# Layer A of a pooling and attention trunk as one stream of units on four PSUM banks

## The chip, the cores and the metric

One core of a Trainium2 chip runs the whole program. The metric is the device time of one execution in microseconds (us). The engines are TensorE (PE, matmuls; PEld is its weight load), VectorE (DVE), ScalarE (ACT), GpSimd (POOL) and SyncE (SP), which issues nearly all DMAs in the order of its queue.

## What is computed

x has 512 positions of 2048 channels. Layer A is a gated pooling mixer, layer B is latent attention on the residual stream. What the change touches is layer A and the norms at the start of layer B:

```python
def pool_mixer_layer(x, norm_g, w_in, w_group, scale, w_out):
    h = rmsnorm(x, norm_g)
    proj = h @ w_in                                   # 2048 -> 2 * 4096
    u, gate = proj[..., :W_A], proj[..., W_A:]
    u = u.reshape(B, S, N_POOL_GROUPS, G_A)           # 4 groups of 1024
    pooled = jnp.stack([causal_mean_pool(u[:, :, gi], w) - u[:, :, gi]
                        for gi, w in enumerate(POOL_WINDOWS)], axis=2)   # windows 2, 4, 8, 16
    y = jnp.einsum('bsgc,gcd->bsgd', pooled, w_group).reshape(B, S, W_A) * scale
    y = y * jax.nn.silu(gate)
    return x + y @ w_out                              # 4096 -> 2048
```

Layer B normalises the new x (shared_kv, mla_layer): an rmsnorm of x, and one each of the key and value latent and of the query latent, both 512 wide.

## The kernel before

Channels lie on the 128 partitions, positions along the free axis; a tile is 128 x 512 in float32. Every float32 operand is split into a rounded high part (a cast on ACT) and a low remainder (a subtraction on DVE), and a product is three matmuls: high by high, high by low, low by high (`mm3`, `split`).

**Seven products for eight.** The products with `w_in` and `w_out` are made for pairs of output tiles by a scheme with seven block products in place of eight. `w_combos` (L278) loads the two weights of a pair for two input pairs (512 KB), forms the sums on DVE (L283) and POOL (L285, L286), casts seven blocks on ACT (L289) and subtracts on DVE (L290). `seven` (L300) issues 21 matmuls of 256 columns for each input pair (L306, L308, L310) into four PSUM banks `k0` to `k3`. `gather` (L313) sums the banks (ACT L317, DVE L318 to L321). The inputs stand split in eight tiles `xh`, `xl`, one for each pair of input tiles, in the pool `xcp`.

**Stages of layer A**, one after the other:
1. A first stage loads x, splits it and multiplies pairs 16 and 17 of the 32 output pairs.
2. The other pairs go in the order `early + late` (L410), four `w_combos` each. Pairs 0 to 15 are u, 16 to 31 the gates. Pairs 18 to 21 go before the norm factor `r2` is known and are stored raw. A pair of u is scaled by `r2` and pooled at once for pairs 0 to 11 (`pool_pair`, one doubling step after the other on DVE, L337, then L343, L344, and a store to DRAM); pairs 12 to 15 are stored and pooled later. Gates go through SiLU and to DRAM. `finish_gates` does that for pairs 16 to 21 later, behind the pools of pairs 0 to 5.
3. `group(g, j0)` (L455) multiplies one pooling group with its own matrix: eight steps, each with a DMA of 512 KB of weights and one of 256 KB of pooled data, a split of 128 x 1536 and 24 matmuls of 512 columns into all eight banks. Then y = product by scale by gate (L477), its block sums (L483 to L485) and splits, as the next `xh`, `xl`.
4. Groups 0 and 1, then the output pass b = 0 over eight pairs (`out_part`, `out_end`): it adds the product to the residual and stores it (L510, L512); pools 12 to 15 are spread over it. Then groups 2 and 3 and the pass b = 1. Each pass starts with the first halves of pairs 0 and 1.

The tiles of weights (`raw` with three buffers, `hi` and `lo` with two) are shared by all these stages.

**Layer B** begins with products of the new x. `norm_r` (L165) makes a norm factor: four float32 products with one column of ones, reciprocal square root by three Newton steps on 128 x 4 (`rsqrt`, L156), then a diagonal matrix and a product that spreads it over the partitions.

**Order.** The program is written as one sequence. A planner orders the instructions of each engine by its own estimate of when each could run, with the written order as priority; so an instruction may be moved ahead of one that waits. Within an engine's queue the result is fixed.

Of the kernel before, what the change touches and what calls it, by code (L numbers as in the profile page):

```python
# [7 lines left out]
F32 = mybir.dt.float32  # L8
# [6 lines left out]
P = 128  # L15
# [36 lines left out]
def trunk_kernel(  # L52
# [128 lines left out]
    def r_tile():  # L181
        return rpool.tile([P, S], F32, tag="r", name="r")
# [56 lines left out]
    tile_ = dict(reuse_waits="tile")  # L239
# [3 lines left out]
    with ExitStack() as c1:  # L243
# [83 lines left out]
        def pool_pair(pair, up, nt):  # L327

            w = WINS[pair // 4]
            G.memset(up[:, :, 0:PAD], 0.0)  # L330
            prev, off = up, PAD
            m = 1
            while m < w:
                ext = w - 2 * m
                nw = S + ext
                nx = nt()
                V.tensor_tensor(nx[:, :, 0:nw], prev[:, :, off - ext:off + S],  # L337
                                prev[:, :, off - ext - m:off + S - m], ALU.add)
                prev, off = nx, ext
                m *= 2  # L340

            rc = cs[:, None, C_RCNT:C_RCNT + w - 1].broadcast_to([P, 2, w - 1])
            V.scalar_tensor_tensor(prev[:, :, 0:w - 1], prev[:, :, 0:w - 1], float(w), rc, ALU.mult, ALU.mult)  # L343
            V.scalar_tensor_tensor(prev[:, :, 0:S], prev[:, :, 0:S], 1.0 / w, up[:, :, PAD:],  # L344
                                   ALU.mult, ALU.subtract)
            raws[pair] = dram()
            nc.sync.dma_start(raws[pair], prev[:, :, 0:S])
# [40 lines left out]
        c3 = ExitStack()  # L388
        tp[0] = c3.enter_context(tc.tile_pool(name="tpool1", bufs=3, **tile_))
        rp = c3.enter_context(tc.tile_pool(name="rp", bufs=1, **tile_))  # L390
# [17 lines left out]
        early = (18, 19, 20, 21)  # L408
        late = (22, 0, 8, 23, 1, 9, 24, 2, 10, 25, 3, 11, 26, 4, 12, 27, 5, 13, 28, 6, 14, 29, 7, 15, 30, 31)
        for n, pair in enumerate(early + late):  # L410
            ks = banks()
            for q in range(NJ // 2):
                w = w_combos(*(awin[2 * pair + m][:, q * S:(q + 1) * S] for m in range(2)))
                seven(ks, w, 2 * q)
                seven(ks, w, 2 * q + 1)
# [3 lines left out]
            if n == 4:  # L419
                V.tensor_tensor(sq[:, 0, :], sq[:, 0, :], sq[:, 1, :], ALU.add)  # L420
                p = ps7.tile([P, 2, H], F32, tag="k3", name="k3").rearrange("p h t -> p (h t)")
                norm_r(sq[:, 0, :], D, p, pt()[:, 0, 0:S], [(r2[:, 0, :], 1.0), (r2[:, 1, :], -1.0)])
            v = gather(ks)
            if n < 4:
# [3 lines left out]
            elif pair < 12:  # L428
                up = pt()
                V.tensor_tensor(halves(up[:, :, PAD:]), v, halves(r2), ALU.mult)  # L430
                pool_pair(pair, up, pt)
                if pair < 6:
                    finish_gates(16 + pair)
# [580 lines left out]
```

## Time and profile before

| | us |
|---|---|
| median of three runs (lowest, highest) | 1974.17 (1972.12, 1975.93) |
| the profiled execution | 1973.28 |
| its span | 1971.5 |
| granted TensorE clock, mean | 0.996 |
| PE busy | 1915.2 |
| DVE busy | 1423.4 |
| ACT busy | 853.6 |
| POOL busy | 508.1 |

The profile gives each engine's busy time, the idle time before groups of instructions and what ended it, the waits of one engine for another, the chain of waits that ended last, and busy times by stretches of the span. A stretch is a row with start and end, its length, for each of PE, PEld, DVE, ACT and POOL the busy time and the count of instructions, then the granted clock, the DMA engines' busy share and GB/s. Matmuls are pipelined and their ends are modelled: a stretch's count of matmuls against its length tells more than its busy time.

### The profile page before, as it was taken

The numbers are of one execution on the slowest core, as the hardware profiler recorded it, in microseconds if no ns is written. First come the engines' busy times: TensorE is split into PE (matmuls) and PEld (weight loads), VectorE is DVE, ScalarE is ACT, GpSimd is POOL, SyncE is SP. The second block draws the span as 40 slices with busy tenths as digits, with TensorE's granted clock in tenths as the row PEclk, the third lists the DMA queues.
The fourth block names the chain that finished last, engine by engine and source line by source line (L and its number), as shares of the span: only waits on it lengthen the run. The fifth ranks groups of instructions, "written<-read, shape, count | busy, mean of one in ns | idle before, by whom it ended". The sixth has DMA issues, their size and how long they took to land.

```text
span 1971.5 us, 32773 instructions
## 1 busy us (share of the span) xinstructions
PE 1915.2 (97%) x12540; PEld 1753.3 (89%) x12540; DVE 1423.4 (72%) x2198; ACT 853.6 (43%) x1435; POOL 508.1 (26%) x516
## 2 busy tenths in 40 slices
PE   8999999999999999899998999999999999999999
PEld 7999999999999988899788998888888888888887
DVE  8767899998988667898478877663344788797332
ACT  7533333334333334333243335543253777785221
POOL 0434554554454105443015330000010111110000
PEclk9999999999999999999999999999999999999999
DMA  6643444535444563455654444322222111121632
GB/s 197 212 131 124 144 144 146 161 129 161 140 140 128 162 215 126 139 193 185 205 165 128 161 150 149 126 89 96 97 92 84 45 48 38 59 65 49 217 120 86
DMA packets 217294, 258.73 MB, mean 131 GB/s; under 512 B 14385, under 2 KB 155569, under 8 KB 217137
## 3 DMA queue, kind: packets, MB, share of 16 engines
q1 hardware_dynamic: 216848, 256.43, 40.4%
q8 instruction: 98, 1.61, 0.4%
q14 instruction: 60, 0.48, 0.1%
q10 hardware_dynamic: 288, 0.20, 0.0%
HBM read 221.98 MB, written 34.60 MB: 130 GB/s over the span
## 4 chain that ended last, share of the span: by engine, by line
PE 73%; DVE 10%; DMA 6%; issue 4%; ACT 4%; POOL 2%; SPq 0%; DVEq 0%; POOLq 0%; ACTq 0%
PE k L310 11%; PE k L308 10%; PE k L306 10%; PE mm L145 7%; PE mm L143 7%; PE mm L144 7%; DVE lo L290 4%; DMA raw<-awo 3%; PE k L143 2%; PE k L144 2%; PE k L145 2%; DMA raw<-awin 2%; PE sc L805 2%; PE mm L679 1%; POOL raw L285 1%
## 5 line engine op out<-in xcount | busy, mean ns | idle before, releaser
L308 PE MATMUL k<-xl,hi 128*128 128x256 f32 x2576 | 707.5, 284 | 5.8 <-DVE xl L149 5.8
L306 PE MATMUL k<-xh,hi 128*128 128x256 f32 x2576 | 705.9, 284 | 7.2 <-ACT hi L289 4.3
L310 PE MATMUL k<-xh,lo 128*128 128x256 f32 x2576 | 645.9, 285 | 13.1 <-DVE lo L290 13.1
L289 ACT CAST hi<-raw 128x1792 fp32r<-128x1792 f32 x184 | 311.6, 1694 | 570.8 <-PE k L310 297.4
L306 PEld LDWEIGHTS k<-xh,hi 128*128 128x128 f32 x2576 | 494.4, 192 | 10.5 <-ACT hi L289 6.1
L308 PEld LDWEIGHTS k<-xl,hi 128*128 128x128 f32 x2576 | 496.5, 193 | 6.7 <-DVE xl L149 6.5
L290 DVE TENSOR_TENSOR lo<-raw,hi 128x1792 fp32r<-128x1792 f32 x184 | 404.2, 2197 | 103.9 <-ACT hi L289 103.7
L310 PEld LDWEIGHTS k<-xh,lo 128*128 128x128 f32 x2576 | 456.5, 192 | 19.8 <-DVE lo L290 18.9
L285 POOL TENSOR_TENSOR raw<-raw 128x256 f32<-128x256 f32 x184 | 225.0, 1223 | 708.8 <-DVE raw L283 498.2
L126 DVE TENSOR_TENSOR wlo<-raw,whi 128x512 fp32r<-128x512 f32 (+2 forms) x213 | 138.6, 657 | 172.2 <-ACT whi L125 167.5
L286 POOL TENSOR_TENSOR raw<-raw 128x256 f32<-128x256 f32 x184 | 232.9, 1266 | 14.4
L125 ACT CAST whi<-raw 128x512 fp32r<-128x512 f32 (+2 forms) x213 | 124.7, 597 | 250.2 <-PE mm L144 210.2
L283 DVE TENSOR_TENSOR raw<-raw 128x512 f32<-128x512 f32 x184 | 138.2, 751 | 48.1 <-DMA raw<-awin 28.3
L144 PE MATMUL mm<-bt,whi 128*128 128x512 f32 x348 | 136.3, 392 | 0.0
L145 PE MATMUL mm<-bt,wlo 128*128 128x512 f32 x348 | 136.0, 391 | 0.2 <-DVE wlo L126 0.2
L143 PE MATMUL mm<-bt,whi 128*128 128x512 f32 x348 | 136.2, 391 | 0.0
L144 PE MATMUL k<-lo,hi 128*128 128x512 f32 x256 | 99.8, 390 | 1.7 <-DVE lo L149 1.7
L145 PE MATMUL k<-hi,lo 128*128 128x512 f32 x256 | 99.7, 389 | 0.0
L149 DVE TENSOR_TENSOR lo<-raw,hi 128x1536 fp32r<-128x1536 f32 x32 | 56.0, 1756 | 52.9 <-ACT hi L148 48.9
L148 ACT CAST hi<-raw 128x1536 fp32r<-128x1536 f32 x32 | 47.2, 1481 | 97.5 <-PE k L145 65.8
L145 PEld LDWEIGHTS mm<-bt,wlo 128*128 128x128 f32 x348 | 65.3, 188 | 14.6 <-DVE wlo L126 0.6
L144 PEld LDWEIGHTS mm<-bt,whi 128*128 128x128 f32 x348 | 65.3, 188 | 14.2 <-issue 0.7
(818 smaller groups left out, 3061.8 us busy)
## 6 DMA issues: line engine op xcount, KB each, us to landing
raw<-awin SPq DMA_DIRECT2D x240, 256.0 KB, 3.2
raw<-awo SPq DMA_DIRECT2D x128, 256.0 KB, 3.1
raw<-bwin SPq DMA_DIRECT2D x80, 256.0 KB, 2.5
scr<-tp SPq DMA_DIRECT2D x32, 512.0 KB, 3.2
raw<-awg SPq DMA_DIRECT2D x32, 512.0 KB, 4.0
raw<-bwo SPq DMA_DIRECT2D x59, 256.0 KB, 2.6
raw<-scr SPq DMA_DIRECT2D x32, 256.0 KB, 4.3
y<-scr SPq DMA_DIRECT2D x32, 256.0 KB, 4.5
```

The lines of the kernel that those rows point to most:

```text
L126: V.tensor_tensor(lo[:, :n], raw[:, :n], f(hi[:, :n]), ALU.subtract)
L143: T.matmul(dst, wh, xh, start=first, stop=False)
L144: T.matmul(dst, wh, xl, start=False, stop=False)
L145: T.matmul(dst, wl, xh, start=False, stop=last)
L283: V.tensor_tensor(c[:, :, 4:6, :], c[:, :, 0:1, :].broadcast_to([P, 2, 2, P]), c[:, :, 1:3, :], ALU.add)
L285: G.tensor_tensor(c[:, :, 6, :], c[:, :, 4, :], c[:, :, 2, :], ALU.add)
L286: G.tensor_tensor(c[:, :, 7, :], c[:, :, 6, :], c[:, :, 3, :], ALU.add)
L289: A.copy(hi, c[:, :, 1:8, :])
L290: V.tensor_tensor(lo, c[:, :, 1:8, :], f(hi), ALU.subtract)
L306: T.matmul(dst, hi[:, j % 2, wi, :], xh[j][:, xi, :], start=first, stop=False, skip_group_check=True)
L308: T.matmul(dst, hi[:, j % 2, wi, :], xl[j][:, xi, :], start=False, stop=False, skip_group_check=True)
L310: T.matmul(dst, lo[:, j % 2, wi, :], xh[j][:, xi, :], start=False, stop=last, skip_group_check=True)
```

## The change

Layer A becomes one written sequence of units that each use four banks (two units alternate on the eight).

- A unit is a pair of input products (`in_pair`) or half a group (`group_half(g, h)`: four of the eight outputs, eight steps of 12 matmuls; the step loads 256 KB of weights and 256 KB of pooled data and splits 128 x 1024). Each half loads the pooled data anew.
- The halves of groups 0 and 1 stand among the input pairs. Groups 2 and 3 stand before the two output passes as before, in halves.
- y of groups 0, 1 and 2 goes to DRAM (`ydram`), and is loaded again by `y_parts`, which makes the block sums and splits. y of group 3 stays in its tiles (`keep`).
- Work of DVE that isn't urgent is put in a list `later` with a price in us: the doubling steps of the pools (1.25 each) and their ends (1.5), the six late gates (1.25), the two parts of `y_parts` (1.6 and 2.2), the rope tables (6.0). `spare(us)` after each product block (2.0) or group step (1.4) gives credit, up to 8, and emits what the credit pays; gathers and scalings take credit away. `until(mark)` emits all up to a mark where the result is needed.
- Pairs 12 and 13 are pooled directly like 0 to 11; 14 and 15 during the first output pass.
- Temporary tiles of layer A have five buffers in one pool for all of it, in place of three in the first half and a pool `pp` for the second.
- In layer B `norm_r` is replaced by `norm_wide` in three places: one product with a 128 x 128 matrix of ones gives the sum on all partitions, and scaling and `rsqrt` run on 128 x 512. Three small constants move to a pool opened after layer A.

```diff
+    def norm_wide(acc, n):
+        p = tr()
+        T.matmul(p, ones, acc, start=True, stop=True)
+        v, a = tt_(), tt_()
+        r = rpool.tile([P, S], F32, tag="r", name="r")
+        V.tensor_scalar(v, p, 1.0 / n, EPS, ALU.mult, ALU.add)
+        rsqrt(v, r, a, S)
+        return r
...
+        def spare(us):
+            credit[0] = min(credit[0] + us, 8.0)
+            while later and later[0][0] <= credit[0]:
+                us, work = later.pop(0)
+                credit[0] -= us
+                work()
+        def until(mark):
+            while any(w is mark for _, w in later):
+                us, work = later.pop(0)
+                credit[0] -= us
+                work()
...
             m = 1
             while m < w:
+                later.append((1.25, lambda m=m: double(m)))
                 m *= 2
+            later.append((1.5, end))
+            return marker()
...
+        def product(ks, w, q, us=2.0):
+            seven(ks, w, 2 * q)
+            seven(ks, w, 2 * q + 1)
+            spare(us)
...
+        def group_half(g, h, keep=False):
+            for pair in range(4 * g, 4 * g + 4):
+                until(pooled[pair])
+            acc = banks()
             for k in range(8):
+                raw = w7.tile([P, 8, P], F32, tag="raw", name="raw", bufs=3)
...
                 split(raw, hi, lo)
+                for o in range(4):
                     mm3(acc[o].rearrange("p h t -> p (h t)"), hi[:, o, :], lo[:, o, :], x, k == 0, k == 7)
+                spare(1.4)
+            if keep and h:
+                until(ready[5])
+            for o in range(4):
...
                 V.scalar_tensor_tensor(y, acc[o], cs[:, col:col + 1], y, ALU.mult, ALU.mult)
+            credit[0] -= 3.0
+            if keep:
+                return ys
             for i, y in enumerate(ys):
+                d = dram()
+                ydram[4 * g + 2 * h + i] = d
+                nc.sync.dma_start(d.rearrange("p m t -> p (m t)"), y.rearrange("p m t -> p (m t)"))
+        def y_parts(j, i, y=None):
...
+            later.append((1.6, sums))
+            later.append((2.2, parts))
+            return marker()
...
+        for unit in (18, 19, 20, 21, 22, 0, 8, 1, 23, 2, 9, 3, 24, 10, (0, 0), 4, 12, 25, 5, (0, 1), 11, 6, 26, 13,
+                     7, 27, 14, (1, 0), 28, 15, 29, (1, 1), 30, 31):
+            if isinstance(unit, tuple):
+                group_half(*unit)
+            else:
+                in_pair(unit)
+        until(marker())
+        for j in range(NJ):
+            ready[j] = y_parts(j, j)
+        group_half(2, 0)
+        group_half(2, 1)
+        out_pass(0)
+        until(marker())
+        for j in range(4):
+            ready[j] = y_parts(j, 8 + j)
+        for h in range(2):
+            ys = group_half(3, h, keep=True)
+            for i, y in enumerate(ys):
+                ready[4 + 2 * h + i] = y_parts(4 + 2 * h + i, None, y)
+        out_pass(1)
...
-        r = norm_r(ac, 512, tr(), tt_(), [(r_tile(), 1.0)])
+        r = norm_wide(ac, 512)
...
-    rb[0] = norm_r(accs[0], D, tr(), tt_(), [(r_tile(), 1.0)])
+    rb[0] = norm_wide(accs[0], D)
```

In `out_part`, `until(ready[j])` stands before the first product that uses part j. `y_parts` loads y from `ydram` in its `sums`, which also makes the block sums of L483 to L485; its `parts` holds the two splits.

More of the change, by code (lines that the diff above doesn't have):

```diff
@@ L441, in trunk_kernel @@
                 silu_pair(pair, halves(pt()[:, :, 0:S]), v, halves(r2))
[L442 to L464 removed]
+        ydram = [None] * 16
```

197 lines of the change are left out of this document (107 added, 90 removed).

## The prediction, made before the changed kernel ran

> **What bounds the kernel now.** I read the page's first lines, then stretches of time cut at the stages of layer A, then the waits of TensorE, then the chain of waits.
>
> ```profile
> span 1971.5 us, 32773 instructions
> PE 1915.2 (97%) x12540; PEld 1753.3 (89%) x12540; DVE 1423.4 (72%) x2198; ACT 853.6 (43%) x1435; POOL 508.1 (26%) x516
> ```
>
> TensorE (PE) is 97% busy, but a busy PE isn't a PE at its peak, so I count matmuls. Two undisturbed stretches of the view by windows (length, then busy time and count for each engine) give the price of one:
>
> ```profile
> 500.00:600.00 100.00, 100.00 (x835) 100.00 (x835) 85.09 (x74) 37.25 (x27) 50.28 (x42) 1.00 0.45 143
> 700.00:736.00 36.00, 36.00 (x160) 29.80 (x159) 24.36 (x26) 15.54 (x13) 0.00 (x0) 1.00 0.59 183
> ```
>
> A 256-column matmul takes 100/835 = 0.120 us, a 512-column one 36/160 = 0.225 us. Now layer A: products of the input pairs, groups 0 and 1, first output pass, groups 2 and 3, second pass.
>
> ```profile
> 55.62:671.81 616.19, 610.98 (x5051) 607.07 (x5050) 516.94 (x453) 236.74 (x176) 292.54 (x248) 1.00 0.47 148
> 671.81:761.13 89.32, 87.53 (x386) 71.82 (x385) 59.81 (x88) 32.70 (x28) 9.14 (x6) 1.00 0.58 185
> 761.13:940.31 179.18, 168.49 (x1345) 164.68 (x1345) 158.80 (x151) 62.57 (x47) 78.07 (x63) 0.98 0.50 164
> 940.31:1032.04 91.73, 88.16 (x387) 71.69 (x385) 57.98 (x59) 31.13 (x25) 9.13 (x6) 1.00 0.59 187
> 1032.04:1205.75 173.71, 165.31 (x1344) 163.03 (x1344) 130.80 (x129) 61.08 (x46) 64.34 (x59) 0.99 0.42 137
> ```
>
> The code issues 5040, 384, 1344, 384 and 1344 matmuls there. Against their price (with 2 us for the norm's ten among the input pairs) the stages lose 616.2 - 603.6 - 2 = 10.6, 89.3 - 86.4 = 2.9, 179.2 - 161.0 = 18.2, 91.7 - 86.4 = 5.3 and 173.7 - 161.0 = 12.7 us: 49.7 us, the most that the rearrangement of layer A can win. Finer stretches say where:
>
> ```profile
> 300.00:671.81 371.81, 371.81 (x3094) 371.31 (x3093) 319.82 (x272) 139.53 (x102) 178.71 (x151) 1.00 0.46 146
> 761.13:811.13 50.00, 43.15 (x320) 41.22 (x321) 42.45 (x44) 20.52 (x17) 25.18 (x16) 0.93 0.37 112
> 811.13:940.31 129.18, 125.34 (x1027) 123.46 (x1026) 116.34 (x108) 42.05 (x30) 52.89 (x47) 1.00 0.56 184
> 1032.04:1090.00 57.96, 50.25 (x386) 48.02 (x386) 48.75 (x51) 24.07 (x20) 29.66 (x19) 0.97 0.38 123
> 1090.00:1205.75 115.75, 115.06 (x958) 115.02 (x958) 82.05 (x79) 37.01 (x27) 34.69 (x40) 1.00 0.44 144
> ```
>
> The same sum gives 1.1 us after 300 us (so nearly all 10.6 fall before it), 11.7 at the head of the first pass and 6.1 in its rest, 11.7 and 1.0 in the second. The two heads are one event. TensorE's waits in the first head, and the chain's longest pieces there:
>
> ```profile
> PE k L308 <- DVE xl L149: 2.9, 2, 2.6
> PE k L306 <- ACT hi L289: 1.8, 3, 0.8
> PE k L310 <- DVE lo L290: 1.7, 3, 0.8
> PE k L306 <- DVE y L477: 0.9, 1, 0.9
> ...
> 767.80 8.21 POOL raw L285
> ```
>
> The groups end, their y is scaled and split on DVE in a burst, the output weights' sums wait behind it on DVE and POOL, and PE waits for both.
>
> **The change, part by part.** These groups carry the prices (last: mean ns of one before the bar):
>
> ```profile
> L290 DVE TENSOR_TENSOR lo<-raw,hi 128x1792 fp32r<-128x1792 f32 x184 | 404.2, 2197 | 103.9 <-ACT hi L289 103.7
> L283 DVE TENSOR_TENSOR raw<-raw 128x512 f32<-128x512 f32 x184 | 138.2, 751 | 48.1 <-DMA raw<-awin 28.3 <-DMA raw<-awo 19.5
> L149 DVE TENSOR_TENSOR xl<-ts,xh 128x1024 fp32r<-128x1024 f32 x16 | 22.1, 1382 | 0.3 <-ACT xh L148 0.3
> L276 DVE TENSOR_TENSOR xl<-raw,xh 128x1024 fp32r<-128x1024 f32 x8 | 9.8, 1224 | 1.1 <-ACT xh L275 1.1
> L149 DVE TENSOR_TENSOR xl<-y,xh 128x768 fp32r<-128x768 f32 x16 | 15.1, 954 | 0.0
> L483 DVE TENSOR_TENSOR ts<-y 128x512 f32<-128x512 f32 x16 | 11.8, 739 | 0.3
> L484 DVE SCALAR_TENSOR_TENSOR ts<-ts,y 128x256 f32<-128x256 f32 x16 | 8.7, 543 | 0.3
> L485 DVE SCALAR_TENSOR_TENSOR ts<-ts,y 128x256 f32<-128x256 f32 x16 | 6.7, 421 | 0.3
> L477 DVE SCALAR_TENSOR_TENSOR y<-k,cs,y 128x512 f32<-128x512 f32 x32 | 21.8, 743 | 0.0
> L148 ACT CAST xh<-ts 128x1024 fp32r<-128x1024 f32 x16 | 16.7, 1044 | 10.4 <-DVE ts L485 10.4
> ```
>
> *Matmuls of layer A*: the same number and shapes; 0.
>
> *Input pairs.* Pooling, six late gates and the two pools of pairs 12 and 13 are emitted piecewise. A product of 42 matmuls takes 5.04 us; its own DVE work is 0.75 + 2.20 = 2.95, so 2.1 are free, and the code deals out 2.0. Of the 9.5 us lost before 300 us some is the start of the stream, which stays. Between 0 and -9.5 I take -2: after 300 us the same density without dealing out lost 1.1.
>
> *Groups in halves.* A step falls from 24 to 12 matmuls, 5.4 to 2.72 us, its split from 1536 to 1024 elements (1.04 ACT, 1.22 to 1.38 DVE). With two buffers the cast starts when the step before last ends and both take 2.3 to 2.4 us: that fits in 2.72, with less cover than before. In all these are 64 casts of 1.04 = 67 us on ACT (43% busy) and 64 by 1.3 = 83 us on DVE (72% busy), each for 2.72 us of matmuls. What shows is each entry (gather and step 1 both want DVE), each inner seam and each exit. Before, entries looked like this:
>
> ```profile
> PE k L143 <- ACT hi L148: 0.9, 1, 0.9
> PE k L144 <- DVE lo L149: 1.7, 2, 1.3
> ```
>
> The first group entry cost 0.9, the second 0.9 + 1.7 = 2.6; mean 1.75. There are now six entries from products (four halves in the stream, 2 and 3 once each): 10.5. Two inner seams at 0.9: 1.8. Four exits into input pairs at 0.9, the wait on L477's row, though its cause goes (a unit now has four banks and the next the other four): 3.6. Together 15.9 for 8.2 before: +7.7. Ends: 0 added, and +23 at 2.6 an entry, 1.7 a seam and 3 an exit.
>
> *Heads of the passes.* Part of the burst moves ahead. Eight y parts cost 0.74 + 0.54 + 0.42 + 0.95 + 1.22 to 1.38 = 3.87 to 4.04 us each, 31.0 to 32.3. Free on DVE until they are needed: 16 steps by 2.72 less 1.22 to 1.38 (24.0 to 21.4), less eight L477 (5.9), and five products by 2.09 (10.4): 28.5 to 25.9. They are short by 2.5 to 6.4, mean 4.4, and with 0.9 for the exit a head loses 5.3 in place of 11.7. In the first pass's rest 2 pools in place of 4: 1.0 for 6.1, as in the second pass. Together 12.6 for 30.5 (11.7 + 6.1 + 11.7 + 1.0): -17.9. Ends: -25 (2.5 a head, all exits hidden) and -5 (heads as before).
>
> POOL bears on this: its adds stand in the chain of every output weight. Their price (least, median, most ns), and the stretch of the longest:
>
> ```profile
> L285 POOL TENSOR_TENSOR raw<-raw x184: 731/742/8214, 45.1 to 1190.3; 128x256 f32<-128x256 f32 x184
> 767.80:776.00 8.20, 7.56 (x61) 7.36 (x62) 7.62 (x8) 1.07 (x2) 8.20 (x1) 1.00 0.34 106
> ```
>
> The median is 0.74 us; the one of 8.21 ran while DVE was busy for 7.62 of 8.20 us. [...]
>
> *y through DRAM.* Twelve stores and twelve loads of 512 KB and 32 second reads of 256 KB of pooled data. SP's queue issues in order, so behind a store of y that waits for L477, or of a pool that now ends later, stand the next weight loads; three raw buffers, some 8 us of steps, cover that. The rate:
>
> ```profile
> 690.20:739.50 49.30, 49.30 (x220) 40.80 (x219) 30.93 (x32) 18.80 (x16) 0.00 (x0) 1.00 0.69 216
> raw<-awg SPq DMA_DIRECT2D x9, 512.0 KB, 4.2
> raw<-scr SPq DMA_DIRECT2D x9, 256.0 KB, 4.5
> y<-scr SPq DMA_DIRECT2D x8, 256.0 KB, 5.9
> ```
>
> 216/0.69 = 313 GB/s is full. Both halves of group 2 ask 8.4 MB of steps, 2.1 of gates, 2.1 of stores and 3.1 of six y loads: 15.7 MB or 50.2 us in 43.5. So +0 to +6.7; I take +2, since gates load ahead and the last store comes after.
>
> *norm_wide*, three in layer B: eight 1-column matmuls go, 0.8 us each time (they start 0.1 us apart):
>
> ```profile
> L170 PE MATMUL tr<-ones,tt__12435 x8: 166/250/251, 1262.9 to 1263.6; 128*128 128x1 f32 x8
> L126 DVE TENSOR_TENSOR wlo<-raw,whi 128x512 fp32r<-128x512 f32 (+2 forms) x213 | 138.6, 657 | 172.2 <-ACT whi L125 167.5
> ```
>
> -2.4. Its twelve DVE operations become 512 wide, 12 by 0.66 = 7.9 us; the latent projections on PE cover them. Without that cover: up to +7.9 each. Moving the rope tables and the constants' pool: 0, DVE has room in the first pass.
>
> **Sum:** -2 + 7.7 - 17.9 + 2 - 2.4 = -12.6. The profiled execution took 1973.28 us (span 1971.5), 0.9 under the median of 1974.17. Forecast 1960.7, say 1961.
>
> **Rivals.**
> *All seams hidden.* Group terms 0, heads at their low end: -25 - 2 - 2.4 = -29, 1944 us. For it: the quiet 300 to 672 us; against it: every entry and head so far waited.
> *POOL starved at the heads.* DVE is now full through groups 2 and 3, so the first output weights' sums wait as at 767.80: heads 11.7 again, +12.8 on the forecast, 1974: no change. It decides once DVE runs without gaps for about 8 us there. Against it: half of the y parts are then done.
> *Slower: landings set the step.* A raw buffer's round is landing + 1.04 + 1.38 + about 0.8 of issue and handoffs, and must fit three steps, 8.16 us: it decides from 5.0 us of landing. At the 5.9 of L475's row the round is 9.1, 3.04 a step; 0.32 by 64 steps = +20, and 1981. For it: two requests each 2.72 us and stores beside them; against it: half-sized weight loads should land before 4.2.
>
> **How the numbers follow.** Forecast 0.45 (1952 to 1968), hidden seams 0.18, starved POOL 0.16, slow landings 0.21. Measurement tells 0.2%, 4 us. Faster is the first two, 0.63; same the third, 0.16; slower the last, 0.21. The range leaves about a tenth out at each end: 1943 (just under the hidden case) to 1984 (just over the slow one).
>
> **What the changed profile would show.** Right: counted as above, output passes lose 13 us for 31 and the eight halves some 16 above 174 us of matmuls; no wait of PE over 2 us at a head; no tr matmuls of one column. Wrong: a POOL L285-like add of 8 us at a head; ACT's cast in a half waiting for DMA at most steps; DMA share over 0.85 in group 2; waits of PE after the norms in layer B.

## The result, and the profile after

The changed kernel is slower, by 1%. It takes 1994.26 us (median of four runs, 1991.39 to 1997.27) where the kernel before takes 1973.94 us (also four) on the same chip: a ratio of 1.0103, 95% interval 1.0085 to 1.0121. The forecast was 1961 us. The profiled execution took 1993.49 us with a span of 1991.7, 20.2 longer than before; its granted clock is 0.991 (0.996 before). The page's first lines, after:

```profile
span 1991.7 us, 33037 instructions
PE 1920.7 (96%) x12516; PEld 1755.2 (88%) x12516; DVE 1445.5 (73%) x2227; ACT 871.2 (44%) x1464; POOL 465.8 (23%) x516
```

No engine's busy time has moved by more than some 40 us, and PE's only by 5.5, so the loss can't be read here. Stretches cut at the units can. In order: the input pairs before the first half; then a half of group 0 or 1 and the input pairs behind it, four times in turn; group 2 in halves; the first pass; group 3 in halves; the second pass; layer B.

```profile
55.34:351.95 296.61, 286.75 (x2364) 284.02 (x2362) 241.62 (x219) 117.19 (x90) 129.08 (x115) 1.00 0.50 164
351.95:377.30 25.35, 21.95 (x99) 17.85 (x97) 20.49 (x23) 9.39 (x10) 3.31 (x5) 1.00 0.65 214
377.30:462.57 85.27, 83.91 (x673) 83.41 (x673) 67.38 (x57) 28.14 (x20) 38.12 (x30) 0.96 0.41 134
462.57:487.12 24.55, 22.49 (x99) 17.69 (x97) 18.53 (x21) 9.33 (x9) 2.37 (x5) 1.00 0.67 218
487.12:633.13 146.01, 143.36 (x1176) 142.75 (x1177) 125.39 (x106) 50.50 (x36) 74.53 (x56) 0.99 0.41 133
633.13:656.93 23.80, 22.54 (x99) 17.70 (x97) 14.53 (x16) 9.34 (x9) 3.27 (x4) 1.00 0.70 225
656.93:719.27 62.34, 60.82 (x504) 60.61 (x505) 40.52 (x36) 21.13 (x15) 17.78 (x21) 1.00 0.44 143
719.27:745.62 26.35, 23.99 (x99) 19.01 (x98) 14.38 (x16) 10.40 (x10) 3.61 (x4) 0.94 0.61 204
745.62:789.43 43.81, 42.03 (x337) 41.83 (x336) 26.12 (x23) 14.10 (x10) 10.62 (x13) 0.96 0.43 143
789.43:844.51 55.08, 46.45 (x194) 35.16 (x192) 47.87 (x61) 29.20 (x31) 4.18 (x4) 1.00 0.88 290
844.51:1013.66 169.15, 165.59 (x1344) 164.18 (x1345) 153.60 (x157) 63.66 (x50) 62.50 (x62) 0.98 0.53 174
1013.66:1065.01 51.35, 46.18 (x194) 36.69 (x192) 38.40 (x49) 23.91 (x25) 4.23 (x4) 0.97 0.70 226
1065.01:1228.97 163.96, 163.11 (x1344) 162.85 (x1344) 123.25 (x116) 57.61 (x42) 56.86 (x60) 0.99 0.44 144
1228.97:1991.70 762.73, 744.52 (x3724) 628.81 (x3722) 469.00 (x1262) 387.86 (x1049) 49.52 (x128) 1.00 0.28 93
```

I count as the prediction does, 0.1198 us for a matmul of 256 columns (603.6/5040) and 0.225 for one of 512, with the counts that the code issues (2352, 96, 672, 96, 1176, 96, 504, 96, 336, 192, 1344, 192, 1344). A half of four outputs is then worth 21.6 us, and the loss of each stretch is its length less its matmuls. "Exits" are the input pairs behind the four halves.

| loss above the matmuls, us | before | forecast | after |
|---|---|---|---|
| input pairs, first stretch (2 us for the norm taken off) | 10.6 | 8.6 | 12.8 |
| groups 0 and 1, after in halves (3.8 + 3.0 + 2.2 + 4.8) | 2.9 | 7.0 | 13.7 |
| exits of these halves (4.8 + 5.1 + 2.0 + 3.6) | | 3.6 | 15.4 |
| groups 2 and 3 (11.9 + 8.2) | 5.3 | 5.3 | 20.0 |
| all groups and exits | 8.2 | 15.9, and 2 for y through DRAM | 49.1 |
| output passes (8.1 + 3.0 after) | 30.9 | 12.6 | 11.1 |

Against before that is +2.2, +40.9 and -19.8; behind the second pass the span is 3.0 shorter and its start 0.3 earlier: 20.0 in all, for a span that grew by 20.2. (The prediction's 30.5 for the passes before is the sum of its finer stretches.) A stretch ends where the next unit's first matmul starts, so the wait for that unit's first weights stands in the row of the half: 3.4, 2.0 and 0.8 of the 13.7 us, and 3.5 and 1.4 of the 20.0. A half is best read together with its exit, 29.1 us in four. So the passes gained what was forecast, and the groups in halves lost more than that. TensorE's longest waits:

```profile
PE k L316 <- DVE lo L296: 17.0, 17, 2.4
PE k L312 <- ACT hi L295: 15.4, 9, 3.5
...
PE k L144 <- DVE lo L149: 6.8, 7, 2.4
PE k L143 <- ACT hi L148: 4.7, 4, 2.3
```

L312 and L316 (L306 and L310 before) stand for the product blocks. Before, the casts and remainders of product weights cost PE 4.3 and 13.1 us, never over 1.2 at a time:

```profile
PE k L310 <- DVE lo L290: 13.1, 22, 1.2
...
PE k L306 <- ACT hi L289: 4.3, 7, 0.8
```

**One exit, followed.** The queue of SP at the end of half (0, 0), then the engines that the product's weights pass through (start, length, engine, line):

```profile
363.64 1.86 SPq L518 DMA_DIRECT2D tp<-scr  x4
365.59 3.40 SPq L288 DMA_DIRECT2D raw<-awin  x4
...
372.76 0.69 DVE L289 TENSOR_TENSOR raw<-raw 128x512 f32<-128x512 f32 x1 [1.95 <-DMA raw<-awin]
...
373.67 0.72 POOL L291 TENSOR_TENSOR raw<-raw 128x256 f32<-128x256 f32 x1 [6.99 <-DVE raw L289]
374.47 1.05 POOL L292 TENSOR_TENSOR raw<-raw 128x256 f32<-128x256 f32 x1
...
375.56 3.27 ACT L295 CAST hi<-raw 128x1792 fp32r<-128x1792 f32 x2 [6.00 <-POOL raw L292]
...
377.30 0.38 PE L312 MATMUL k<-xh,hi 128*128 128x256 f32 x1 [3.40 <-ACT hi L295]
```

The landing times of L288's loads (the product weights) from 300 to 340 us, and then at this exit:

```profile
DMA to landing us min/median/max: 2.8/3.2/3.5
...
DMA to landing us min/median/max: 2.9/5.3/6.6
```

The four loads of gates (L518, 1 MB together) are issued at 363.64, the first load of weights at 365.59. PE's last matmul of the half starts at 373.51, so the weights have 7.9 us from issue to use. They need a landing, 0.69 on DVE, 0.72 and 1.05 on POOL and a cast of 1.7: some 4.5 us with handoffs behind the landing. With an undisturbed landing of 3.2 that is 7.7, and the second load of the block is issued 0.4 us after the first: it just fits, with nothing to spare. Behind the gates the block's two loads land 6.4 and 6.6 us after their issue, DVE sits until 372.76, some 7 us after the first issue, and PE stops for 3.40 us. The stop then costs more, as the granted clock shows in the stretches behind it:

```profile
377.30:382.30 5.00, 4.41 (x21) 4.11 (x22) 4.75 (x4) 1.53 (x1) 2.06 (x1) 0.55 0.78 291
377.30:400.00 22.70, 22.11 (x160) 21.81 (x161) 12.92 (x11) 6.60 (x4) 9.42 (x8) 0.85 0.40 137
```

The 160 matmuls are worth 19.2 us and take 22.7; the only other wait there is one of 0.6, so 2.9 us go to a clock that is granted at 0.55 for the first five. With the two waits the exit loses about 6.9 us, where the prediction had 0.9: a row that it took from a wait of another cause.

### The profile page after: what moved, and what is told of

Read it like the earlier page. It is cut to its first block, busy times and chain, and to the rows that moved or that the text cites. A ratio compares the mean times of both kernels' runs of the same rounds, so it can differ in the third digit from the quotient of the medians.

```text
span 1991.7 us, 33037 instructions
## 1 busy us (share of the span) xinstructions
PE 1920.7 (96%) x12516; PEld 1755.2 (88%) x12516; DVE 1445.5 (73%) x2227; ACT 871.2 (44%) x1464; POOL 465.8 (23%) x516
## 4 chain that ended last, share of the span: by engine, by line
PE 76%; DVE 11%; DMA 5%; ACT 4%; issue 3%; SPq 1%; POOL 0%; DVEq 0%; ACTq 0%; POOLq 0%
PE k L316 13%; PE k L312 12%; PE k L314 12%; PE mm L143 7%; PE mm L145 7%; PE mm L144 7%; DVE lo L296 4%; DMA raw<-awin 2%; PE sc L911 2%; PE mm L785 2%; PE mm L786 1%; PE mm L787 1%; DVE lo L149 1%; PE k L144 1%; DMA raw<-awo 1%
## 5 line engine op out<-in xcount | busy, mean ns | idle before, releaser
L312 PE MATMUL k<-xh,hi 128*128 128x256 f32 x2576 | 710.9, 285 | 15.4 <-ACT hi L295 15.4
L316 PE MATMUL k<-xh,lo 128*128 128x256 f32 x2576 | 647.9, 286 | 17.2 <-DVE lo L296 17.0
L295 ACT CAST hi<-raw 128x1792 fp32r<-128x1792 f32 x184 | 310.9, 1691 | 574.9 <-PE k L316 321.0
L312 PEld LDWEIGHTS k<-xh,hi 128*128 128x128 f32 x2576 | 498.5, 194 | 18.7 <-ACT hi L295 18.3
L316 PEld LDWEIGHTS k<-xh,lo 128*128 128x128 f32 x2576 | 460.1, 194 | 21.8 <-DVE lo L296 21.6
L291 POOL TENSOR_TENSOR raw<-raw 128x256 f32<-128x256 f32 x184 | 194.5, 1057 | 731.3 <-DVE raw L289 564.2
L292 POOL TENSOR_TENSOR raw<-raw 128x256 f32<-128x256 f32 x184 | 220.7, 1199 | 14.2
L149 DVE TENSOR_TENSOR lo<-raw,hi 128x1024 fp32r<-128x1024 f32 x64 | 78.1, 1221 | 57.1 <-ACT hi L148 57.0
L148 ACT CAST hi<-raw 128x1024 fp32r<-128x1024 f32 x64 | 67.3, 1051 | 105.0 <-PE k L145 51.3
L144 PEld LDWEIGHTS mm<-bt,whi 128*128 128x128 f32 x348 | 65.3, 188 | 14.2 <-issue 0.7
```

The source lines that it names most:

```text
L144: T.matmul(dst, wh, xl, start=False, stop=False)
L291: G.tensor_tensor(c[:, :, 6, :], c[:, :, 4, :], c[:, :, 2, :], ALU.add)
L292: G.tensor_tensor(c[:, :, 7, :], c[:, :, 6, :], c[:, :, 3, :], ALU.add)
L295: A.copy(hi, c[:, :, 1:8, :])
L312: T.matmul(dst, hi[:, j % 2, wi, :], xh[j][:, xi, :], start=first, stop=False, skip_group_check=True)
L316: T.matmul(dst, lo[:, j % 2, wi, :], xh[j][:, xi, :], start=False, stop=last, skip_group_check=True)
```

## The experiments

My theory after this (B in the quoted expectations): a step of half the width leaves the weight loads too short a lead, so that whatever is queued ahead of them shows as a wait of PE. Its rivals: the order of the loads at a half's end alone; the burst of late gates; the scalings on DVE (E); the dealing out of DVE's work; the mixing as such; the new norms. The expectations call theories by letters; each says what its theory means for that run. The kernels ran on several chips, on which the kernel before took 1974 to 1976 us, so ratios to it are compared: 0.001 is 2.0 us, and the changed kernel stands at 1.0103.

**Single parts undone or moved.** *Loads of gates, scalings and stores of a half issued behind the second weight load of the next unit:*

```diff
-            for o in range(4): ... gate loads, scalings ...; for i, y in enumerate(ys): ... store
+            tails.append([2, tail])    # called after the second w_combos or group step that follows
```

> The changed kernel (1994 us) with one thing moved: the gate loads, scaling and y stores at the end of each half of groups 0, 1 and 2 are issued behind the second weight load of the unit that follows (group 3 as before). Theory A: four gate loads of 256 KB go out just before the next unit's first weights, which then land after 6.2 to 6.6 us in place of 3.2, and PE waits at each exit; of the 28 us that the four halves in the stream and the heads behind them lose, 10 to 16 go, and group 2 gains 1 to 3: 1977 to 1984. Theory B: the exits lose because three raw buffers give 8 us of lead to a chain of load, DVE sum, POOL sums, cast and remainder that needs 9 whatever else is loaded: at most 4 us go, 1990 to 1994.

1990.52 us, ratio 1.0078 (1.0061 to 1.0095). The half above and the pairs behind it, in this kernel:

```profile
353.73:376.34 22.61, 21.95 (x99) 17.84 (x97) 18.86 (x21) 9.34 (x9) 3.33 (x5) 1.00 0.60 194
376.34:461.48 85.14, 83.00 (x672) 82.39 (x673) 69.47 (x59) 28.35 (x20) 40.12 (x31) 0.98 0.45 147
```

The half loses 1.0 in place of 3.8, its exit 4.6 in place of 4.8: the wait of 3.40 is gone, others stand behind it. The four halves and exits together lose 22.3 in place of 29.1, group 2 loses 14.2 in place of 11.9, and the whole gains only some 5 us, with an interval that overlaps that of the changed kernel. The order at the seam is part of the cause and not most of it.

*No gates loaded at all* (y is then scaled by the norm factor in place of the gate):

```diff
-                nc.sync.dma_start(y, z.rearrange("p (h t) -> p h t", h=2))
-                V.scalar_tensor_tensor(y, acc[o], cs[:, col:col + 1], y, ALU.mult, ALU.mult)
+                V.scalar_tensor_tensor(y, acc[o], cs[:, col:col + 1], halves(r2)[:, 0], ALU.mult, ALU.mult)
```

> The changed kernel without the gate loads: y is the product by scale by the norm factor, the gate is left out of it, all else stays (same DVE instruction with another operand). 8 MB of 277 fewer. Theory A: exits lose 1 us or less each, and group 2, whose stretch had the DMA engines 94% busy, loses half of its 11.6 us: 1968 to 1980. Theory B: exits as in the changed kernel, group 2 a little better: 1988 to 1994.

1983.39 us, 1.0037 (1.0024 to 1.0051): 13 us. These 8 MB weigh more than their order does: the four halves and exits lose 17.2 in place of 29.1. The kernel stays slower than before without them, so they aren't all of it. Group 2 hardly gains, though its DMA share falls from 0.88 to 0.75:

```profile
779.77:833.14 53.37, 46.96 (x194) 34.86 (x193) 46.42 (x58) 29.08 (x30) 4.70 (x4) 1.00 0.75 241
```

It still loses 10.2 us, so a high share of the DMA engines isn't by itself what group 2 loses by.

*The six late gates one for each pair, in place of one burst:*

```diff
-                for g in range(6):
-                    later.append((1.25, lambda g=g: finish_gates(16 + g)))
+            if 5 <= n < 11:
+                later.append((1.25, lambda g=n - 5: finish_gates(16 + g)))
```

> The changed kernel with the six late gates (512 KB load and 512 KB store each) put into the list one behind each of six pairs, as the kernel before had them, in place of all six at once. PE loses 6.3 us from 150 to 250 us in the changed kernel, where these loads stand ahead of weights in the queue. Theory A (bursts of data ahead of weights): that falls to 2 us or less, total 1989 to 1991. Theory B: the start of the stream is short of DVE time, and spreading the gates does nothing: 1993 to 1995.

1994.49 us, 1.0098 (1.0083 to 1.0113): no effect beyond the measurement.

*The scalings too behind the next unit's second remainder* (on top of the first experiment):

```diff
-                    with tc.issue_after(lastdma[0].ins):
+                    with tc.issue_after(lastdma[0].ins), tc.issue_after(lastlo[0].ins):
```

> The changed kernel with gate loads behind the next unit's second weight load, as in the first of these runs (0.25% under the changed kernel), and DVE's four scalings of y (0.74 us each) put behind the remainder of that unit's second block, too. In that first run the exits still waited 0.8 to 1.3 us for the first cast and 1.2 to 3.0 us for its remainder, while DVE ran the scalings. Theory E, the scalings stand ahead of the remainder in DVE's queue: 6 to 10 us less than 1990, 1980 to 1984. Theory B, load, sums and cast come too late by themselves: 1988 to 1991.

1993.08 us, 1.0089 (1.0075 to 1.0103). No gain over the first experiment (the exit of half (0, 0) loses 5.1 in place of 4.6). The theory that the scalings alone hold up the exits (E) falls.

*The old norms in the changed kernel, and the new norms in the kernel before:*

```diff
-        r = norm_wide(ac, 512)
+        r = norm_r(ac, 512, tr(), tt_(), [(r_tile(), 1.0)])
```

> The changed kernel with the three norms of layer B narrow again (128x4 Newton steps, one-column matmuls). By the prediction's term the wide norm saves 2.4 us: 1996.7. Layer B's part of the two traces (763.5 us before, 758.9 after) says 4.6: 1998.9. If the difference there comes from the moved pools and not from the norm: 1994.

> The kernel before with the wide norm in layer B alone. The narrow norm put back into the changed kernel cost about 2.5 us. If the norm is worth the same here: 2 to 5 us under the kernel before on the same chip; if the gain needs the changed kernel's layout of layer B: within 1 us of it.

1998.29 us, 1.0116 (1.0101 to 1.0132), and 1971.94 us, 0.9988 (0.9979 to 0.9997). The first interval overlaps that of the changed kernel; the second lies just under 1. Both points give 2.4 to 2.6 us for the wide norms, the term of the prediction (2.4).

*No metering: everything in the list is emitted at the next occasion:*

```diff
-            credit[0] = min(credit[0] + us, 8.0)
+            credit[0] = 1e9
```

> The changed kernel with unlimited credit: all listed work of DVE is written right behind the next product or step, nothing is dealt out. If dealing out is worth something (theory A takes it as the part that works): 3 to 10 us slower, 1997 to 2004. If the planner spreads DVE's work by itself: 1992 to 1996. Theory D, dealing fills DVE's gaps so that POOL's adds and the remainders come late: faster, under 1990.

2000.32 us, 1.0128 (1.0113 to 1.0143). Dealing out helps, by some 5 us: the intervals overlap, but in the profiled executions the first pass loses 13.3 us without it, for 8.1.

**Width and place.** *Whole groups on eight banks in the same mixed stream, y still through DRAM:*

```diff
-            acc = banks()
+            acc = [b for _ in range(2) for b in banks()]
-                for o in range(4):
+                for o in range(8):
-                     7, 27, 14, (1, 0), 28, 15, 29, (1, 1), 30, 31):
+                     7, 27, 14, 28, 15, 29, (1,), 30, 31):
```

> The changed kernel with whole groups in place of halves: all eight banks, eight steps of 24 matmuls, weights and pooled data loaded once (768 KB per 5.4 us in place of 512 KB per 2.72), group 0 where the half (0,1) stood, group 1 where (1,1) stood, groups 2 and 3 ahead of their passes; y through DRAM, dealing out and wide norms stay. Theory A (the halves' short steps: three raw buffers give 8 us of lead in place of 16, and 192 GB/s of step loads leave no room for gates and y): the groups and the heads behind them lose 10 to 15 us in place of 47, and the total is 1960 to 1972, under the kernel before. Theory C (each change between kinds of units costs, whatever the step): half as many seams, 1983 to 1988.

1981.57 us, 1.0033 (1.0020 to 1.0046). Groups 0, 1 and 2, and the second pass:

```profile
435.36:481.64 46.28, 44.01 (x194) 35.80 (x193) 24.32 (x22) 13.54 (x10) 8.30 (x7) 1.00 0.57 175
685.18:731.42 46.24, 44.05 (x194) 35.78 (x193) 20.48 (x18) 14.47 (x11) 8.17 (x6) 1.00 0.56 175
773.44:820.16 46.72, 44.07 (x194) 35.76 (x192) 39.37 (x49) 24.68 (x24) 10.68 (x4) 1.00 0.76 239
1041.64:1221.29 179.65, 167.26 (x1344) 164.82 (x1345) 133.37 (x150) 63.22 (x51) 62.94 (x59) 0.98 0.41 136
```

Groups lose 3.1, 3.0 and 3.5 us, where the halves of groups 0 and 1 lost 6.7 and 7.0 and those of group 2 11.9. Group 2 takes its 43.2 us of matmuls at a DMA share of 0.76 in place of 0.88. The two exits lose 2.3 and 1.8, and all groups and exits 18.8 in place of 49.1. Against that the first pass loses 12.1 (8.1 in the changed kernel), and the second, with the first wait of layer B in its row, 18.6 (by the same measure 6.8), since the parts of group 3 have no second half to lie under. So the halves are what costs, and what they buy lies at the head of a pass. The total lies between the two ranges of the expectation and nearer to that of the seams (C): the run has fewer seams as well as wider steps, and it doesn't tell the two apart.

*All input pairs first, then the six halves of groups 0 to 2 in a row:*

```diff
-        for unit in (18, ... 10, (0, 0), 4, 12, 25, 5, (0, 1), ... (1, 0), 28, 15, 29, (1, 1), 30, 31):
+        for unit in (18, ... 10, 4, 12, 25, 5, ... 28, 15, 29, 30, 31, (0, 0), (0, 1), (1, 0), (1, 1)):
```

> The changed kernel with all input pairs first and then the halves (0,0), (0,1), (1,0), (1,1), (2,0), (2,1) in a row. Four exits into input pairs and three entries go. Theory A: the exits' 25 us go, but six halves in a row ask for more than the DMA engines move, and each loses 3 to 6 us as those of group 2: 1988 to 1998. Theory C: seams are the cost, 1975 to 1982.

1977.58 us, 1.0009 (1.0000 to 1.0019): 19 us under the changed kernel. Input pairs, then the six halves:

```profile
56.19:680.24 624.05, 613.48 (x5051) 609.98 (x5050) 529.25 (x465) 236.22 (x176) 296.88 (x249) 0.99 0.45 146
680.24:832.31 152.07, 141.45 (x578) 109.17 (x576) 102.52 (x116) 66.38 (x66) 3.44 (x5) 0.97 0.86 281
```

The pairs lose 18.4 (28.2 with the exits before), the six halves 22.5 (25.5): of the 15.5 us between the two profiled executions 9.8 lie in the pairs, where the four exits are gone, and 3.0 in the halves. The range of the theory of the seams (C) held, that of its rival (A) didn't. The halves still lose, now at a DMA share of 0.86.

**The lead of the loads.** *Four raw buffers in place of three, so that each weight load is issued a block earlier; one gather tile in place of two, to make room:*

```diff
-                raw = w7.tile([P, 8, P], F32, tag="raw", name="raw", bufs=3)
+                raw = w7.tile([P, 8, P], F32, tag="raw", name="raw", bufs=4)
-        epool = c1.enter_context(tc.tile_pool(name="epool", bufs=2, **tile_))
+        epool = c1.enter_context(tc.tile_pool(name="epool", bufs=1, **tile_))
```

> The changed kernel with four raw buffers in place of three and, to make room, one gather tile in place of two. Theory B (at an exit the next unit's load, sums and cast have too short a lead behind short steps): one more buffer lets the first load go 2.72 us sooner, and the exits' 28 us fall by 6 to 12: 1982 to 1988, 0.4 to 0.7% over the kernel before. If DVE's and the DMA engines' backlog sets the exits: no change or slower, 1.0% or more over.

1979.18 us, 1.0021 (1.0011 to 1.0031). No work is taken away and nothing is reordered by hand, and 16 of the 20 us are back. The first stretch, the four halves and group 2:

```profile
54.83:345.64 290.81, 286.23 (x2363) 283.92 (x2362) 243.46 (x218) 117.75 (x91) 132.96 (x112) 1.00 0.51 166
345.64:367.89 22.25, 22.10 (x99) 17.95 (x97) 18.79 (x19) 9.35 (x9) 4.61 (x5) 1.00 0.68 223
453.58:476.78 23.20, 21.95 (x99) 17.85 (x97) 19.08 (x21) 9.34 (x9) 4.49 (x5) 1.00 0.73 232
621.77:645.71 23.94, 22.08 (x98) 17.95 (x97) 15.75 (x17) 9.34 (x9) 4.82 (x5) 1.00 0.66 212
707.78:732.86 25.08, 22.67 (x98) 18.38 (x97) 16.33 (x18) 10.40 (x10) 5.36 (x6) 0.97 0.67 208
774.30:831.28 56.98, 48.83 (x202) 37.50 (x201) 49.01 (x58) 29.84 (x31) 6.91 (x5) 0.97 0.83 275
```

5.8 us come back in the first stretch and 8.8 in the four halves and their exits: 8.1 lost for 13.7 in the halves, where the waits at their ends stand, and 12.2 for 15.4 in the exits. That is inside the 6 to 12 of the expectation, and most of the exits' loss is still there. At the exit followed above PE no longer waits for the cast but for the remainder. The remainder could start when its cast ends, at 366.65; in DVE's queue it stands behind the sum of a later block, which waits for its load, and behind two scalings:

```profile
PE k L316 <- DVE lo L296: 3.3, 1, 3.3
...
367.98 0.73 DVE L289 TENSOR_TENSOR raw<-raw 128x512 f32<-128x512 f32 x1 [1.50 <-DMA raw<-awin]
...
369.96 2.30 DVE L296 TENSOR_TENSOR lo<-raw,hi 128x1792 fp32r<-128x1792 f32 x1
```

So at this exit the lead is one part of the loss, and the order of DVE's queue behind it another, which no run with four buffers changed. Group 2, whose row holds eight matmuls of the pass, still loses 12.8: the longer lead doesn't help there.

*The same two edits (four raw buffers, one gather tile) in the kernel before:*

> The kernel before with the same two edits alone: four raw buffers, one gather tile. If the lead of the loads is short in general (Theory B in its wide form), the two heads of layer A, the start of the stream and the passes lose less, and the kernel is 5 to 12 us under before (0.994 to 0.997). If it is particular to the narrow units of the mixed stream, it stays within 2 us of before (0.999 to 1.001), or is slower by what one gather tile costs.

1970.15 us, 0.9974 (0.9964 to 0.9983): 5.1 us, at the low end of the range given for a general shortage. The gain lies in the input pairs (6.4 lost for 10.6); groups and passes lose what they lost, and the heads were not helped. So of the 16 us some 5 were to be had before as well, and the other 11 belong to what the change added.

*The same two edits in the un-mixed kernel:*

> e8 (all input pairs first, then the six halves of groups 0 to 2 in a row; 1.0009 of before) with the four raw weight buffers and one gather tile of e14. If un-mixing (17 us under the changed kernel) and the longer lead (16 us) each take a loss of their own, both together give 0.993 to 0.996 of before. If they are two cures of one loss (weight loads that come late where a half meets an input pair), the pair is hardly better than either alone: 0.998 to 1.002 of before.

1963.83 us, 0.9956 (0.9939 to 0.9972), 10.5 us under the un-mixed kernel and 29 under the changed one. Were the two edits independent, it would be 0.9927; were they one cure, 1.000. They are mostly two: un-mixing takes the exits away, and the longer lead gives 7.3 us back in the input pairs (11.1 lost for 18.4) and 5.4 in the six halves (17.1 for 22.5).

**Towards a kernel that beats both.** *The un-mixed stream, groups 0 and 1 whole, 2 and 3 in halves:*

```diff
-            if isinstance(unit, tuple):
-                group_half(*unit)
+            if isinstance(unit, tuple):          # ... 30, 31, (0,), (1,)
+                group_whole(*unit)               # as in the kernel with whole groups
```

> The changed kernel's stream of input pairs with dealt pools, then groups 0 and 1 whole, then halves of groups 2 and 3 and the passes as in the changed kernel. Against the unmixed run (0.09% over the kernel before) four halves that lost some 12 us become two whole groups that lose 5: 5 to 8 us less, 1969 to 1973 on the same scale. Theory C alone (only seams count): 1974 to 1977.

1967.54 us, 0.9963 (0.9951 to 0.9975): 9 us under the un-mixed kernel, a little more than the 5 to 8 expected.

*As that, with the order, the immediate pools and the three temporary tiles of the kernel before in the stream, and pools 12 to 15 dealt out under groups 0 and 1:*

```diff
+        for late in (12, 13, 14, 15):
+            pool_late(late)
         group_whole(0)
         group_whole(1)
```

> Input pairs in the order and with the immediate pools of the kernel before (pairs 12 to 15 stored); then groups 0 and 1 whole with y to DRAM, pools 12 to 15 dealt out under their long steps; then as in the changed kernel: y parts under the halves of group 2, first pass, halves of group 3, second pass, wide norms. Theory A and C together (halves and mixing lose, early y parts and the wide norm win): input pairs lose 10 as before, the two whole groups 5, group 2 and the first pass 16, group 3 and the second pass 13, layer B 2.4 less: 4 to 9 us under the kernel before, 1966 to 1971 on a chip where that takes 1975. If the dealt stream is what the heads need: not under the kernel before.

1976.20 us, 1.0003 (0.9994 to 1.0012): a miss, with one wait of PE behind group 0, since the loads of its gates want tiles that the dealt pools still hold:

```profile
PE k L143 <- DVE tp L558: 13.1, 1, 13.1
```

*Pools 12 and 13 under group 0, 14 and 15 under group 1, and the list emptied at step 5 of a group:*

```diff
                 spare(2.8)
+                if k == 5:
+                    until(marker())
```

> The run with the stream as before (equal to the kernel before) waited once for 13.1 us between the whole groups 0 and 1: the scaling of y waited for gate loads, and these for buffers that the dealt pools still held. Here pools 12 and 13 go under group 0 and 14 and 15 under group 1, and the list is emptied before each group's last two steps; all else as there. If that wait was only the buffers': 12 to 15 us less, 1961 to 1965 where the kernel before takes 1975. If the pools under the groups are themselves too much for DVE: 1970 to 1976.

1965.29 us, 0.9947 (0.9935 to 0.9959): 11 us less, so most of that wait is gone, and 10.5 us under the kernel before.

*Two variants of it: five temporary tiles in the stream in place of three; and group 0's parts of y under group 1, for which pool 14 goes under group 0 too and a step of a group gives more credit:*

```diff
-        tp[0] = c3.enter_context(tc.tile_pool(name="tpool1", bufs=3, **tile_))
+        tp[0] = c3.enter_context(tc.tile_pool(name="tpool1", bufs=5, **tile_))
```

```diff
-                spare(2.8)
+                spare(3.4)
...
+        pool_late(14)
         group_whole(0)
-        pool_late(14)
         pool_late(15)
+        for j in range(4):
+            ready[j] = y_parts(j, j)
         group_whole(1)
         until(marker())
-        for j in range(NJ):
+        for j in range(4, NJ):
```

> As the one ahead of it, with five temporary buffers in place of three during the stream of input pairs (order, immediate pools and all else as there). The input pairs lose 10 us with the order and the three buffers of the kernel before, and 17 to 19 in every kernel with the changed stream. If the buffers make that (more loads of x and of gates are let go ahead of weights): 5 to 8 us slower than with three. If it is order or dealing: within 2 us.

> As the run with the list emptied early, with the first four y parts (group 0) under the long steps of group 1 instead of under the halves of group 2, where loads had the DMA engines some 90% busy and DVE was short of time. If group 2 and the first head lose for that reason (10 and 6 us there): 4 to 8 us less than that run. If group 1 then overflows: the same or slower.

1967.09 us, 0.9961 (0.9949 to 0.9974), and 1974.73 us, 0.9992 (0.9983 to 1.0001). The first is not told from its base. In the second the scalings (L560) come late behind the parts, the same mistake as with the pools:

```profile
PE k L143 <- DVE tp L560: 8.6, 2, 5.1
```

*The best of these with the same two edits, four raw buffers and one gather tile:*

> e12 (before's order in the stream, pools 12 to 15 dealt under groups 0 and 1, groups 2 and 3 in halves, wide norms; 0.9947 of before) with four raw weight buffers instead of three and one gather tile instead of two, so that each weight load is issued a block earlier. Theory B (the weights' loads have too short a lead wherever a block is 512 columns or narrower) holds here too, though the steps are longer: a few us under e12, 0.991 to 0.993 of before, with the loss in the halves of groups 2 and 3 and at the start of the stream smaller. Its rival (in before's order the lead is long enough, and only the mixed halves need more; the one gather tile then costs a little at the gathers): 0.994 to 0.998 of before.

1962.06 us, 0.9932 (0.9918 to 0.9946), where the kernel before takes 1975.54: the lowest ratio of all, 13.4 us under before. Its interval overlaps that of its base, so the 3 us between them are not shown; it also overlaps that of the un-mixed kernel with four buffers. Groups 0 to 2, first pass, group 3, second pass:

```profile
667.38:811.98 144.60, 134.18 (x578) 107.18 (x577) 116.25 (x136) 55.54 (x51) 5.09 (x8) 1.00 0.83 277
811.98:982.09 170.11, 163.34 (x1345) 162.93 (x1344) 128.22 (x128) 60.77 (x45) 55.40 (x60) 0.98 0.50 165
982.09:1030.41 48.32, 44.97 (x194) 35.51 (x193) 37.68 (x45) 23.89 (x24) 5.09 (x4) 1.00 0.71 228
1030.41:1199.82 169.41, 163.19 (x1345) 162.77 (x1343) 127.67 (x137) 59.96 (x46) 58.70 (x60) 0.99 0.44 142
```

It keeps what the change won at the heads of the passes (9.1 and 8.4 lost, the second with the first wait of layer B in it, for 18.2 and 12.7 before), and pays 15.0 for groups 0 to 2 and 5.1 for group 3.

## Why the prediction was wrong, step by step

- **Groups in halves: the step that failed.** +7.7 was forecast, and +2 for y through DRAM; +40.9 was measured: 29.1 for the four halves in the stream and their exits where 10.6 stood, 20.0 for groups 2 and 3 where 5.3 stood, less the 8.2 before. The failing sentence is "three raw buffers, some 8 us of steps, cover that". The 8 us were right (7.9 at the exit above), but what they must cover there isn't the landing alone: it is the landing and the sums and the cast of a product's weights, some 8 us when nothing is queued ahead. Exits were priced at 0.9 by a wait on L477, "though its cause goes"; that its cause went said nothing on what is late next. A half and its exit cost 7.3 each. Entries and seams were priced by rows of groups whose steps are twice as long. The upper end given, +23, was too low as well. Three edits take parts of the loss away, and these parts overlap: a longer lead (four raw buffers, 16 us, of which 11 are particular to the change), no mixing of halves and pairs (19 us, 29 with both), and whole groups (30 us less in groups and exits, of which the passes give 16 back, 14 in all). So at the exits the lead is part of the cause; at the one followed, the order on DVE is another.
- **y through DRAM.** +2, with +6.7 as the end, by a rate. Group 2 lost 11.9, at the share over 0.85 that was named as the sign of being wrong; 3.5 of it is the wait for the pass's first weights. But the rate isn't shown to be the cause: without the gates, at a share of 0.75, group 2 lost 10.2, and at 0.76, with whole steps, 3.5. Its loads do land late in the changed kernel (medians of 4.2 and 5.3 us, for 2.8 and 3.2 in half (0, 0)), and DVE is busy for 47.9 of the 55.1 us. Which of these sets the loss stays open.
- **Input pairs.** -2 forecast, +2.2 measured: not the burst of late gates (spreading it changed nothing). Four buffers gave 5.8 us back there, but 4.2 in the kernel before as well, so what made the pairs slower than before isn't shown.
- **Output passes: right in the sum.** -17.9 forecast, -19.8 measured; without metering the first pass loses 5 us more, so dealing the work out ahead does what was said. The split is luck in part: 8.1 and 3.0 lost for 6.3 each. No wait of 2 us was to show at a head, though one of 3.5 (cast L295) does, at the first, in the row of group 2; with it and the 1.4 at the second head the passes lose 16.0, for 32.8 before by the same measure.
- **Norms: right.** -2.4 forecast; 2.4 and 2.6 by the two runs, the second not clear of the measurement.
- **The rivals.** POOL was not starved: no add of product weights takes as long as the 8.21 of before (least, median, most):

```profile
L291 POOL TENSOR_TENSOR raw<-raw x184: 719/742/2406, 44.8 to 1213.5; 128x256 f32<-128x256 f32 x184
```

So POOL did not decide the heads here: filling DVE's gaps went with a longest add of 2.41 us (2.61 on the next line, L292). That a DVE without gaps makes an add as long as the 8.21 was the rival's assumption, from that one add; no run tests it alone. The slower rival, landings, had the sign right and the place in part. Over all halves the loads of the steps land in time (medians of 3.0 and 3.5 us, under its 5.0), but in half (1, 1) both medians are 5.2, and PE stops there for 2.3 us. PE's waits for the splits inside groups are 11.5 us (4.7 + 6.8), where the rival gave 20; those for product weights, which it left out, are 32.4 (15.4 + 17.0). It had 0.21.

What stays open: the loss of group 2 in halves, which only whole groups lowered by much, and the 12.2 us that the exits keep with four buffers. How much of the four buffers' gain comes from the one gather tile that goes with them was not separated.

## What to carry to other kernels

When a step is made narrower, count its buffers in microseconds, not in number: the lead of a load is buffers by step time (three by 2.72 us here), and it must cover the landing behind whatever is queued ahead of it (3.2 us undisturbed, 6.4 and 6.6 behind the gates), and every sum and cast between the landing and the first matmul (some 4.5 us); the remainder behind it needs its turn on DVE as well (with four buffers PE waited 3.3 us for it at the exit followed). A seam between two kinds of units is priced by that chain and the queue there, not by the wait that the old seam happened to show (0.9 here, where that exit lost 6.9). When a large win in one stage is swallowed by another, keep the stage that won and put the other back: the wide norms, metered parts and halves only for groups 2 and 3 kept the passes' gain without the mixed stream, 10.5 us under the kernel before with three buffers.

## What the hardware showed that I had not expected

A stop of PE cost more than its length here. Behind a wait of 3.40 us the granted clock was 0.55 for the next 5 us, about 2.9 us more (0.50 from 378.3 to 384.3 us). It was lower behind a shorter wait too: half (1, 1), with a longest wait of 2.3 us, shows 0.80 in the stretch around it (0.50 from 740 to 743 us).

```profile
378.30:384.30 6.00, 5.41 (x26) 5.11 (x25) 4.44 (x4) 0.53 (x1) 3.12 (x3) 0.50 0.64 224
PE k L143 <- ACT hi L148: 2.3, 1, 2.3
736.00:742.00 6.00, 3.85 (x11) 2.75 (x12) 3.05 (x3) 2.10 (x2) 1.23 (x1) 0.80 0.49 156
740.00:743.00 3.00, 3.00 (x8) 2.32 (x8) 1.68 (x2) 0.00 (x0) 2.15 (x2) 0.50 0.62 188
```

Over the whole kernel this is no small part. TensorE's waits in the products and groups of layer A grow from 29.6 to 43.9 us, by 14.3. The mean granted clock falls by 0.005 (0.996 to 0.991), which over 1991.7 us is some 10 us, an estimate from the two rounded means. Together that is about the 23.3 us by which layer A loses more than before: by this estimate some two fifths of the loss is matmuls at the lower clock, not the stops.
